# The planner of background lanes assumes a lower rate of transfers, and a higher least charge for a small one

## The chip, the cores and the metric

The kernel runs on one core of one Trainium2 chip. The metric is the device time of one execution in microseconds, and lower is better. The core has five engines that work side by side, each in the order of its own instruction stream: TensorE (PE, matmuls, with its weight loads PEld), VectorE (DVE), ScalarE (ACT), GpSimd (POOL) and SyncE (SP, which here issues nearly all transfers). Sixteen DMA engines move the data.

## The reference

One inference step of a decoder layer, for a prompt of 1024 tokens and a sample group of 8 x 4 tokens that share the weights (D_MODEL 1024, FF 2816, all f32):

```python
h = rmsnorm(x, ln1)
proj = h @ w_in          # 7432 columns, split into the inputs of three mixers and the gates
oa = attn_fn(aq, ak, av, sinks)                  # window of 128, 8 heads, 2 kv heads
cu, _ = causal_dwconv(sC * sh, sc_prev, sc_conv_w); ob = sB * cu
oc = gated_deltanet(dqkv, dz, da, db, ...)       # chunked delta rule, a recurrence over chunks
gates = sigmoid(gl)                              # three vectors of 1024 per token
merged = gates[0] * (oa @ w_br_a) + gates[1] * (ob @ w_br_b) + gates[2] * (oc @ w_br_c)
x = x + merged @ w_o
up = rmsnorm(x, ln2) @ ffn_up
gate, val = split(causal_dwconv(up, ff_prev, ffn_conv_w))
x = x + (silu(gate) * val) @ ffn_down            # then a last rmsnorm
```

The outputs are the two token groups and the new caches and states of the mixers.

## The kernel before, in words

All 1056 tokens are held with features on the partitions. Every operand of a large matmul is split into two parts of reduced width, high and low (lines 217 and 218), and a product is three matmuls. A plain projection (`proj`, line 325) makes 128 output columns: three groups of 352 tokens, each 24 matmuls into one PSUM bank of the tag `mm`, of which there are three, and then an evacuation. The larger jobs (`Pairs.run`, line 1429) make 256 output columns with seven block products in place of eight; their operands are sums and differences of blocks, built beforehand (for the gates by `h_build`, lines 1812 and 1824).

The work is one list of foreground jobs in an order written out by hand (`ORDER`):

```python
d4 hbd q0 d5 d6 dpairs d7 D0 D2 D8 D10 delta
v k q1 q2 q3 attn_in attn
sc_start c0 h0 c1 b0 h1 c2 b1 h2 c3 b2 h3 sc_end z0 z1 z2 z3 hb b3
g10 g11 g12 g13 g14 less pairs g15 G16 G00 G02 G04 G06 G20 G22 op1 G24 G26
```

Small letters are plain projections. Evacuations: `v`, `k`, `q`, `c` and `g` in line 1203 on ScalarE, `h` in line 1230 and `b` in line 1253 on VectorE, `z` in lines 1464 and 1465 on both. `G` are pair jobs of the gates. After the list come the merge of the branches, w_o, the up projection (22 jobs) and the down projection.

Everything that is no large matmul runs in background lanes: Python generators that issue a few instructions, then yield a condition. The step `delta` starts the lanes of the delta rule. `pass1` (line 796 and around it) makes 8 chunks' matrices and stores their blocks to `blk_d`, `a_d` and `qk_d`; `solve` loads `blk_d` and runs 31 pairs of VectorE instructions, one after the other (lines 828 and 830), with a yield after every eight; `merge` combines the inverses in products up to line 927; `prep` loads a chunk (six transfers of 256 KB), transposes it (lines 965 and 967) and scales it, at most two chunks ahead; `scan` carries the state through the chunks (lines 988 to 1016). `out_norm` follows (lines 605 and 613). Attention is in lanes too (lines 1601 to 1690). `hb` adds `h_build` for the gate pairs, which begins when all eight chunks are prepared and 12 attention parts are done; it ignores the planner's gate. The step `pairs` waits until `h_build` has taken its first buffers, and G16 until it has built all.

The class `Lanes` (lines 76 to 119) decides where in the program each lane step stands. It keeps a planned time `now` and the planned end of the transfers issued so far, `busy`. The helper `dma` (line 178) charges each transfer before it issues it. A foreground job calls `tick` between its matmuls; in the stretch from `rr1` on a plain projection ticks once in two matmuls with 0.36 us (line 330). A tick moves `now` and runs one step of the first lane that may run; while `busy` is more than 8 us ahead of `now` the lanes marked as moving data may not. A lane that waits for its data yields `arrived`, which is true once `now` has passed the planned end of the transfers plus 3.4 us. Where the foreground needs what a lane has not done yet, `until` runs lane steps alone, 0.3 us of planned time each, and without that gate:

```python
def arrived(self):
    return self.after(max(self.busy - self.now, 0) + DMA_US + 0.9)
def tick(self, force=False, us=TICK_US):
    self.now += us
    full = self.busy - self.now > MAX_BUSY_US and not force
```

The planner's times are only used while the program is written; the chip doesn't see them. The instructions are then ordered per engine by a list scheduler, in which a later place in the program is a lower priority, evacuations are moved up by 100 to 200 places, and an instruction whose inputs are not ready lets later ones pass. The order is fixed before the run.

Of the kernel before, what the change touches and what calls it, by code (L numbers as in the profile page):

```python
# [173 lines left out]
def trunk(tc, A, O, cst_d):  # L174
    nc = tc.nc
    bg = Lanes()

    def dma(dst, src, eng=nc.sync):
        n = 4
        for d in dst.shape:  # L180
            n *= d
        bg.transfer(max(0.5, n / 3.6e5))
        eng.dma_start(dst, src)  # L183
    done = {}

# [60 lines left out]

    ident = cp.tile([128, 128], F32, name="ident")
    dma(ident, cst_d[:, K_ID:K_ID + 128])
    ones_r = cp.tile([128, 128], F32R, name="ones_r")
    hot = cp.tile([128, 96], F32R, name="hot")  # L250
# [11 lines left out]
    def w_load(key, src, nk):  # L262
        t = cp.tile([128, 8, 128], F32, name="wr", tag="wr", bufs=2)
        dma(t[:, :nk, :], src, nc.sync)
        wraw[key] = (t, nk)
# [101 lines left out]
    def state_in(src, rows, nct, dst, name):  # L367

        n = rows * nct
        sd = dtile(name, [n, 128])  # L370
        dma(sd.rearrange("(c r) p -> c r p", r=rows), src.rearrange("r (c p) -> c r p", p=128))
        yield sb.room(1)
        full, rest = n // 128, n % 128
        st = sb.take([128, full + 1, 128])
        if full:
            dma(st[:, 0:full, :], sd[0:full * 128, :].rearrange("(i q) p -> q i p", q=128))
        if rest:
            dma(st[0:rest, full, :], sd[full * 128:n, :])
        yield bg.arrived()
        for i in range(full + (rest > 0)):  # L380
            w = 128 if i < full else rest
            ps = bg_ps()
            transpose(ps[:, :w], st[:w, i, :], ident[:w, :w])
            nc.scalar.copy(dst[:, i * 128:i * 128 + w], ps[:, :w])
            yield
        sb.drop()
# [2084 lines left out]
```

## Time and profile before

| | us |
|---|---|
| median of 3 runs (1920.84 to 1924.7) | 1923.15 |
| the profiled execution, its own time | 1918.24 |
| its span, first to last instruction | 1916.4 |
| TensorE busy | 1776.1 |
| VectorE busy | 1222.4 |
| GpSimd busy | 1116.0 |
| ScalarE busy | 825.1 |

Busy times are of the span; engines overlap. Idle time of an engine counts only where the end waits for it. A matmul row gives the time in which the group was busy; since matmuls overlap in the pipeline, the mean of one (334 ns) is longer than the distance between two.

### The profile page before, as it was taken

What the parts mean: (1) busy time and instruction counts of PE and PEld (TensorE: products, weight loads), DVE (VectorE), ACT (ScalarE), POOL (GpSimd) and SP (SyncE); (2) the same over time, 40 slices, a digit from 0 to 9 for tenths busy, and PEclk for the clock granted to TensorE, in tenths of its full rate; (3) what the DMA queues carried; (4) which work ended last, traced back from release to release, by engine and by line L of the source; (5) the groups of instructions that cost most, each with busy time, mean ns of one, the idle gap of its engine ahead of it and who ended that gap; (6) DMA issues with size and microseconds to landing.
All of it is one profiled execution on the core that took longest, in us unless ns stands there. A gap on an engine that the chain in (4) does not pass through costs nothing.

```text
span 1916.4 us, 34346 instructions
## 1 busy us (share of the span) xinstructions
PE 1776.1 (93%) x13006; PEld 1731.0 (90%) x13006; DVE 1222.4 (64%) x2122; ACT 825.1 (43%) x1780; POOL 1116.0 (58%) x1041
## 2 busy tenths in 40 slices
PE   5899989869999998999988899999999999989997
PEld 4799889769999997999987899999999999889997
DVE  5588813473477787411899956778777778764334
ACT  5445511221244543344553445554554454454433
POOL 3255623443332247976668745998887989434542
PEclk8899999987999998999999999999999999999999
DMA  6312697545765543733461343455454343596513
GB/s 221 99 46 90 192 284 217 143 120 134 183 185 158 163 131 97 264 132 117 156 242 64 134 135 129 127 163 177 142 175 147 121 143 131 224 360 194 179 51 108
DMA packets 293302, 300.84 MB, mean 157 GB/s; under 512 B 56516, under 2 KB 224944, under 8 KB 293120
## 3 DMA queue, kind: packets, MB, share of 16 engines
q1 hardware_dynamic: 233648, 261.94, 42.4%
q10 hardware_dynamic: 59488, 36.70, 6.7%
q8 instruction: 102, 1.67, 0.4%
q14 instruction: 64, 0.52, 0.1%
HBM read 205.30 MB, written 95.28 MB: 157 GB/s over the span
## 4 chain that ended last, share of the span: by engine, by line
PE 56%; DVE 18%; DMA 9%; POOL 5%; issue 5%; ACT 4%; SPq 2%; ACTq 0%; DVEq 0%; POOLq 0%
PE mm L325 15%; PE mm L1429 13%; PE bgps L1429 10%; DVE slot L360 2%; SPq L183 2%; PE bgps L2347 2%; PE bgps L2348 2%; PE bgps L2349 2%; PE mm L2348 1%; PE mm L2349 1%; PE mm L2347 1%; DVE bgps L1457 1%; POOL wl L218 1%; DVE slot L218 1%; DVE slot L2007 1%
## 5 line engine op out<-in xcount | busy, mean ns | idle before, releaser
L325 PE MATMUL mm<-slot,wh 128*128 128x352 f32 x1920 | 488.5, 334 | 40.4 <-DVE slot L1253 21.8
L325 PEld LDWEIGHTS mm<-slot,wh 128*128 128x128 f32 x1920 | 345.2, 194 | 47.5 <-DVE slot L1253 22.0
L325 PE MATMUL mm<-slot,wl 128*128 128x352 f32 x960 | 319.5, 333 | 4.0 <-POOL wl L218 4.0
L1429 PE MATMUL mm<-slot,wh 128*128 128x264 f32 x1536 | 213.6, 289 | 15.6 <-DVE bgps L1457 6.3
L1429 PEld LDWEIGHTS mm<-slot,wh 128*128 128x128 f32 x1536 | 199.5, 192 | 20.5 <-DVE bgps L1457 8.2
L1429 PE MATMUL mm<-slot,wl 128*128 128x264 f32 x1464 | 202.9, 288 | 12.3 <-DVE wl L218 4.2
L1429 PEld LDWEIGHTS mm<-slot,wl 128*128 128x128 f32 x1464 | 188.7, 191 | 15.5 <-DVE wl L218 5.0
L218 POOL TENSOR_TENSOR wl<-slot,wl 128x512 fp32r<-128x512 f32 (+1 forms) x116 | 153.4, 1322 | 83.1 <-ACT wl L217 70.4
L325 PEld LDWEIGHTS mm<-slot,wl 128*128 128x128 f32 x960 | 186.3, 194 | 6.5 <-POOL wl L218 4.7
L218 POOL TENSOR_TENSOR wh<-slot,wh 128x512 fp32r<-128x512 f32 (+1 forms) x103 | 133.7, 1299 | 95.9 <-ACT wh L217 76.0
L218 POOL TENSOR_TENSOR slot<-slot 128x512 fp32r<-128x512 f32 (+3 forms) x95 | 136.0, 1436 | 88.4 <-ACT slot L217 88.2
L217 ACT CAST slot<-slot 128x528 fp32r<-128x528 f32 (+4 forms) x212 | 130.6, 638 | 126.4 <-DVE slot L1824 32.5
L218 POOL TENSOR_TENSOR wl<-wr,wh 128x1024 fp32r<-128x1024 f32 x38 | 94.6, 2489 | 144.0 <-ACT wh L217 134.8
L218 DVE TENSOR_TENSOR slot<-slot 128x528 fp32r<-128x528 f32 (+3 forms) x117 | 115.5, 1002 | 90.3 <-ACT slot L217 83.9
L1429 PE MATMUL bgps<-slot,wl 128*128 128x264 f32 x1128 | 154.1, 287 | 8.2 <-POOL wl L218 4.8
L1429 PEld LDWEIGHTS bgps<-slot,wl 128*128 128x128 f32 x1128 | 144.9, 190 | 9.7 <-POOL wl L218 5.0
L1429 PE MATMUL bgps<-slot,wh 128*128 128x264 f32 x1080 | 146.8, 286 | 2.6 <-DVE slot L2007 1.2
L1429 PEld LDWEIGHTS bgps<-slot,wh 128*128 128x128 f32 x1080 | 138.6, 191 | 3.5 <-DVE slot L2007 1.7
L2187 DVE SCALAR_TENSOR_TENSOR bgps<-slot,bgps 128x358 f32<-128x358 f32 x240 | 127.3, 590 | 13.7 <-ACT bgps L2185 13.0
L1429 PE MATMUL mm<-slot 128*128 128x264 f32 x936 | 124.6, 284 | 1.2 <-DVE bgps L1457 0.6
L217 ACT CAST wl<-slot 128x512 fp32r<-128x512 f32 (+1 forms) x128 | 74.2, 583 | 108.0 <-PE bgps L1429 29.2
L1429 PEld LDWEIGHTS mm<-slot 128*128 128x128 f32 x936 | 118.0, 188 | 1.9 <-DVE bgps L1457 0.8
(404 smaller groups left out, 3929.7 us busy)
## 6 DMA issues: line engine op xcount, KB each, us to landing
wr<-in_w_in SPq DMA_DIRECT2D x32, 512.0 KB
g_d<-slot SPq DMA_DIRECT2D x24, 528.0 KB
slot<-g_d SPq DMA_DIRECT2D x24, 528.0 KB
ht_d<-slot SPq DMA_DIRECT2D x44, 264.0 KB
slot<-ht_d SPq DMA_DIRECT2D x44, 264.0 KB
wr<-in_ffn_up ACTq DMA_DIRECT2D x22, 512.0 KB
slot<-in_ffn_down SPq DMA_DIRECT2D x22, 512.0 KB
slot<-in_ffn_up ACTq DMA_DIRECT2D x22, 512.0 KB
```

What stands on the lines that cost most here:

```text
L183: eng.dma_start(dst, src)
L217: nc.scalar.copy(hi, src)
L218: eng.tensor_tensor(lo, src, f32(hi), op=ALU.subtract)
L325: mm(ps[:, :TG], a[:, k, :], b[k][:, cc], start=n == 0, stop=n == last)
L360: nc.vector.scalar_tensor_tensor(out[:, :L], src[:, j:j + L], w(j), out[:, :L], op0=ALU.mult, op1=ALU.add)
L1429: mm(ps, w[:, x + k, :], b[y][:, c0:c0 + HU], start=not n and piece not in NESTED, stop=n == last, skip_group_check=piece in NESTED)
L1457: nc.vector.tensor_tensor(dst, ps, x, op=ALU.add)
L2007: nc.vector.scalar_tensor_tensor((acc if b == 1 else g)[:, cc], g[:, cc], 1.0, ps, op0=ALU.add, op1=ALU.mult)
L2187: nc.vector.scalar_tensor_tensor(ps, cb[:, a + i:b + i], w(i), ps, op0=ALU.mult, op1=ALU.add)
L2347: mm(ps, hi, bh, start=start, stop=False, skip_group_check=True)
L2348: mm(ps, hi, bl, start=False, stop=False, skip_group_check=True)
L2349: mm(ps, lo, bh, start=False, stop=stop, skip_group_check=True)
```

## The change

One line of the helper `dma`. Nothing that is computed, no instruction and no buffer is changed by it; the charge of a transfer of n bytes is.

```diff
@@ -179,7 +179,7 @@
         n = 4
         for d in dst.shape:
             n *= d
-        bg.transfer(max(0.5, n / 3.6e5))
+        bg.transfer(max(0.6, n / 2.8e5))
         eng.dma_start(dst, src)
     done = {}
```

`bg.transfer` is `self.busy = max(self.busy, self.now) + us`.

## Rows read from the trace of the kernel before

**Rows 1.** The page: busy time of engines, and the span in 40 slices.
```profile
PE 1776.1 (93%) x13006; PEld 1731.0 (90%) x13006; DVE 1222.4 (64%) x2122; ACT 825.1 (43%) x1780; POOL 1116.0 (58%) x1041
...
PE   5899989869999998999988899999999999989997
...
PEclk8899999987999998999999999999999999999999
```

**Rows 2.** Waits of TensorE, whole span: us in total, times, longest.
```profile
PE mm L325 <- DVE slot L1253: 21.8, 1, 21.8
PE mm L325 <- ACT slot L1203: 10.9, 2, 8.1
```

**Rows 3.** Table by stretch: length, busy us of PE, PEld, DVE, ACT, POOL, PEclk, DMA share, GB/s.
```profile
219.00:506.00 287.00, 249.28 (x1521) 238.37 (x1520) 117.14 (x240) 63.86 (x137) 111.79 (x100) 0.91 0.70 189
240.00:290.00 50.00, 43.34 (x250) 42.48 (x251) 7.55 (x15) 7.93 (x14) 13.18 (x6) 0.91 0.98 283
...
436.00:480.00 44.00, 44.00 (x267) 43.59 (x266) 10.96 (x22) 6.52 (x12) 15.01 (x14) 0.81 0.62 138
480.00:510.00 30.00, 30.00 (x187) 27.22 (x187) 8.24 (x15) 7.94 (x13) 9.62 (x9) 0.95 0.76 194
506.00:690.00 184.00, 182.69 (x1259) 176.90 (x1260) 134.47 (x255) 83.75 (x215) 56.68 (x40) 1.00 0.59 166
...
720.00:750.00 30.00, 20.52 (x104) 18.72 (x103) 29.93 (x19) 9.84 (x18) 25.48 (x12) 0.81 0.21 73
```

**Rows 4.** Lines 1253, 927, 965 and 1203: where foreground and delta lanes stand.
```profile
502.00 0.49 DVE L1253 TENSOR_TENSOR slot<-mm,slot 128x320 f32<-128x320 f32 x1 [0.93 <-PE mm L325]
511.47 0.53 DVE L1230 TENSOR_TENSOR slot<-mm,slot 128x352 f32<-128x352 f32 x1 [1.30 <-PE mm L325]
...
L927 PE MATMUL bgps<-slot x32: 218/275/275, 502.3 to 505.7; 128*128 128x64 f32 x32
...
L965 PE MATMUL bgps<-ident,slot x32: 270/272/273, 518.9 to 688.5; 128*128 128x128 f32 x32
...
634.75 0.82 ACT L1203 ACTIVATE slot<-mm 128x352 f32<-128x352 f32 x2
687.42 0.47 ACT L1203 ACTIVATE slot<-mm 128x352 f32<-128x352 f32 x1
745.93 1.16 ACT L1203 ACTIVATE slot<-mm 128x352 f32<-128x352 f32 x3
```

**Rows 5.** DMA issues from 219 to 506 us: count, KB each.
```profile
wr<-in_w_in SPq DMA_DIRECT2D x17, 512.0 KB
qkv_d<-slot SPq DMA_DIRECT2D x11, 512.0 KB
slot<-qkv_d SPq DMA_DIRECT2D x19, 256.0 KB
slot<-rows_d SPq DMA_DIRECT2D x17, 256.0 KB
slot<-ssq_d SPq DMA_DIRECT2D x8, 528.0 KB
slot<-raw_d SPq DMA_DIRECT2D x7, 528.0 KB
...
blk_d<-slot SPq DMA_DIRECT2D x32, 16.0 KB
...
a_d<-slot SPq DMA_DIRECT2D x16, 16.0 KB
```

**Rows 6.** Building of the gate operands, and line 325 alone by stretch (PE, PEld, PEclk, DMA).
```profile
689.86 2.45 POOL L1812 TENSOR_TENSOR slot<-slot 128x1056 f32<-128x1056 f32 x1
...
750.61 1.81 DVE L1824 TENSOR_TENSOR slot<-slot 128x528 f32<-128x528 f32 x1
...
219.00:506.00 287.00, 194.87 (x1083) 182.31 (x1083) 0.91 0.70 189
219.00:690.00 471.00, 312.62 (x1741) 288.02 (x1742) 0.95 0.65 180
690.00:750.00 60.00, 35.67 (x205) 34.16 (x204) 0.91 0.31 100
```

**Rows 7.** The solve on VectorE, and waits between 380 and 450 us.
```profile
398.50 0.19 DVE L828 TENSOR_TENSOR slot<-slot 128x31 f32<-128x31 f32 x1 [2.37 <-DMA slot<-blk_d]
...
433.60 0.19 DVE L828 TENSOR_TENSOR slot<-slot 128x31 f32<-128x31 f32 x1
...
DVE slot L828 <- DMA slot<-blk_d: 2.4, 1, 2.4
...
POOL wl L218 <- DMA slot<-a_d: 9.1, 1, 9.1
```

**Rows 8.** Table by stretch, late stages; columns as in group 3.
```profile
1070.00:1680.00 610.00, 589.46 (x4599) 584.68 (x4597) 460.88 (x868) 296.42 (x649) 472.94 (x510) 0.99 0.45 149
1680.00:1900.00 220.00, 215.83 (x1758) 213.81 (x1759) 100.35 (x160) 93.76 (x180) 95.56 (x76) 0.99 0.56 186
```

## The prediction

> **What bounds it now.** I read the page first [rows 1]: TensorE is busy 93% of 1916.4 us, its clock is granted at 9 or better in most slices, and the slices that fall short are the first, those around 240 to 290 and 410 to 480 us, 720 to 770 us, and the last. So time is lost in a few places, and the question is which of them the pacing reaches. The waits of TensorE [rows 2] put the largest single wait, 21.8 us, on the evacuation in line 1253 (VectorE). The table by stretch [rows 3] sizes the rest: from 219 to 506 us TensorE is busy 249.28 of 287 us at a clock of 0.91 (1.0 is 2.4 GHz, a stretch at 1.2 GHz counts as 0.5), from 506 to 690 it is full (182.69 of 184), and from 720 to 750 it is busy 20.52 of 30 while VectorE is busy 29.93.
>
> The order of this program around the change is made ahead of time: every foreground tick moves the planner's clock (0.36 us for two matmuls here, so 12.96 for a projection job of 72) and runs one lane step, but no moving lane while the planned backlog of transfers is over 8 us. That backlog is what the edit makes larger. It changes no instruction, only where lane steps stand among the foreground jobs.
>
> **The change, step by step.** A 528 KB transfer goes from 1.50 to 1.93 planned us, 512 KB from 1.46 to 1.87, 256 KB from 0.73 to 0.94, anything up to 128 KB from 0.50 to 0.60.
>
> *Step 1, how late the delta lanes get.* The delta chain (pass1, solve, merge) ends with line 927 at 505.7 us, in the foreground between the last evacuation of b2 (502.00) and the first of h3 [rows 4]. From the delta step that is 15 jobs, 15 x 12.96 = 194 planned us. The transfers issued in this stretch (56 groups in the view, 289 transfers, 53.8 MB; eight groups stand) [rows 5] cost 218 planned us by the old rule and 273 by the new: 174 of them are small (+0.1 each, +17), the rest adds 37. More transfer time than foreground time means that the gate at 8 us is what admits lanes here, so the 55 us fall mostly on the lanes. The trace doesn't show the gate itself. Upper bound: all 55, and some 15 more in the preparation that follows (48 loads of 256 KB, +0.21 each, and attention's) = 70. Lower bound: the gate is open half the time, 25. I take 45, nearer the upper end, because the sum exceeds the room.
>
> *Step 2, the slack that hides it.* The last preparation (lines 965, 967, at 689 us) stands just behind the third evacuation of g12 (687.42) [rows 4]: from 634.75 to 745.93 there are 18 evacuations in line 1203, six jobs g10 to g15, and this is the ninth. So 24 of the 26 jobs before the step `pairs` are done; two jobs, 25 planned us, are slack. Delays up to that cost nothing: the matmuls of g13 and g14 only change places with lane work. With 45 the planner stands at `pairs` and runs lanes alone for 20 us; all foreground that is left to put beside them is g15, and behind it G16 waits for the same lane h_build.
>
> *Step 3, what the lost cover costs.* From 690 to 750 us the operands of the gate pairs are built (lines 1812 and 1824, 689.86 to 750.61), and TensorE's cover there is 35.67 us of line 325, 205 matmuls, that is g13 to g15 [rows 6]. Put ahead of the preparation, two of the three are gone: 35.67 x 2/3 = 24 us of idle time, if the building takes as long as now (VectorE fills it, [rows 3], so I see no reason for it to shrink much). The 20 planned us ahead of it are 1.4 chunks of the preparation (one per 24.2 us now: 169.6 us from the first to the last line 965, seven steps [rows 4]). Of a chunk's 24.2 us foreground takes 15.5 (117.75 of 182.69 busy us from 506 to 690, line 325 [rows 3, 6]); alone, a chunk runs on its own chain, between 8.7 us (its TensorE work, no idle) and 24.2 (nothing faster, 15.5 idle). I take 4.5 idle, nearer the lower end since most of the chunk's time is foreground, so 6. The wait also brings a low clock: 720 to 750 stands at 0.81 [rows 3], 4 us on 20.52; I take 4 more. Step 3: +34 us, with 0 (delay within the slack) and 35.67 + 2 x 15.5 = 67 as ends.
>
> *Step 4, what comes back.* From 240 to 290 us the DMA engines are at 0.98 and move 283 GB/s; TensorE loses 6.66 us, and 3.9 to a clock of 0.91 [rows 3]. Lanes that ask for less per us should leave that stretch free: -10.6 (0 to -10.6). The 21.8 us wait is a different thing: the solve (lines 828 and 830, 398.50 to 434 us) runs on VectorE without a break because its input landed late (2.4 us waited for blk_d, and GpSimd 9.1 us for a load of a_d [rows 7]), while TensorE had already filled its three banks with b1. With the clock after it (0.81 over 44 us, 8.4, and 0.95 over 30, 1.5 [rows 3]) this place costs 32 us. The edit leaves the four bursts of the solve in consecutive lane steps, so the lump stays, somewhere else in the order; but with DMA less crowded it may come on time. Between 0 and -32 I take a third, -11: the landing is a small part of the lump.
>
> *Step 5, elsewhere.* From 1070 us on the DMA engines are at 0.45 and 0.56 [rows 8], so the larger waits for arrival (0.2 to 0.4 us each) lie under matmuls: 0. If lane work does come late there, the cover is gone and some us go; I allow 5 either way. At the end `drain` ignores the gate: 0, at most 1.
>
> Sum: +34 - 10.6 - 11 = +12 us. The profiled execution took 1918.24 us (span 1916.4), which gives 1930; the median of the runs shown is 4.9 us above that execution, so I forecast **1935** against 1923.15.
>
> The rate itself can be held against the rows: 283 GB/s at 0.98 [rows 3] says that 280 KB per us is what this mix of transfers gets, and that 360 is not reached there. The Trainium skill (DMA: Bandwidth & Descriptors, Specifications) states about 358 GB/s as a core's limit to HBM, which is the old figure. By that, step 4 would be 0, the sum +34 and the time 1957; the measured stretch decides, for it is the mix that is paced.
>
> **Rivals.**
> - *The stall goes.* The solve falls beside a job that ScalarE evacuates, or its input is on time. Then -32 instead of -11, and with the smaller loss of step 3 (one job of cover, 12, +4 clock): 16 - 10.6 - 32 = -27, about 1897 by the median; with step 3 at 34 it is -9, 1914. For it: 32 us stand in one place and the DMA is overfull ahead of it. Against it: solve's steps stay together, and b and h jobs, two in three, need VectorE to evacuate.
> - *Nothing moves.* The delay stays within 25 planned us and the solve's stall stays: within 4 us of 1923.
> - *Full loss.* The wait at `pairs` is 45 planned us, the stall keeps its size: up to 67 - 10.6 = +56, 1979; half way, with 45, 1958. It decides once the gate is shut all through 219 to 506.
>
> **How the numbers follow.** Forecast (slower, own range 1928 to 1950) 0.45; stall gone 0.34; nothing 0.10; full loss 0.11. A difference of 0.2%, 4 us, is about what a measurement of this kernel can tell from none. Faster 0.34, same 0.10, slower 0.56. The range takes in most of the first rival's times and half of the last: 1896 to 1966.
>
> **What would show it.** Right: the last line 967 stands behind the evacuations of g14 rather than g12; TensorE is busy under 15 us of the 30 before the first line 1429; the DMA share around 240 to 290 us falls below 0.9. Wrong: no idle stretch ahead of the first gate pair (the slack was larger than I count), or the wait on line 1253 and the low clock behind it are gone without another VectorE lump in their place, which would make it faster.

## The result, and the profile after

| | us |
|---|---|
| changed kernel, median of 20 runs (1922.83 to 1938.42) | 1932.85 |
| kernel before, median of 20 runs (1914.27 to 1924.7) | 1920.52 |
| ratio, with its 95% interval | 1.0063 [1.0053, 1.0074] |
| the changed kernel's profiled execution | 1923.49 |

The change makes the kernel slower by 12 us. The forecast was +12 (1935 against 1923.15). The profiled execution of the changed kernel is the second fastest of its 20 runs, so its trace, 5.3 us over that of before (1923.49 against 1918.24), shows less than the median's loss; the other 7 us stand in no trace.

The page of the changed kernel: busy time, the span in 40 slices, and what the DMA engines moved.

```profile
PE 1778.9 (93%) x13006; PEld 1732.0 (90%) x13006; DVE 1226.4 (64%) x2122; ACT 826.7 (43%) x1780; POOL 1122.6 (58%) x1041
...
PE   5899999997999974999998899999999999989997
...
PEclk7899999999899986999998999999999999999999
...
GB/s 216 102 47 90 189 273 195 125 172 129 142 179 187 134 130 106 210 193 138 155 201 114 112 146 113 149 128 160 171 142 144 150 128 164 222 354 210 181 52 108
```

Against [rows 1] the work is the same to the instruction (13006 matmuls), but the weak slices have moved: the 6 at 383 to 431 us is a 9, the slice behind it, a 9 before, is a 7, and the two slices from 673 to 769 us, 9 and 8 before, now stand at 7 and 4; the clock's row has its 6 at the last of these. (A slice is 48 us.) The waits of TensorE over the whole span say the same (us in total, times, longest):

```profile
PE bgps L613 <- ACT slot L217: 16.0, 3, 14.2
...
PE mm L325 <- DVE slot L1465: 10.5, 1, 10.5
```

The 21.8 us on line 1253 [rows 2] is gone as such; behind the solve there now stands one of 10.5, on the evacuation of a z job (line 1465). New is 14.2 us on line 613, the sums of `out_norm`. That is lane work; the wait ends at 748.93 us, and TensorE runs nothing in it, no foreground either. The table by stretch (columns as in [rows 3]) sizes both places.

```profile
219.00:506.00 287.00, 268.08 (x1663) 258.92 (x1662) 137.66 (x264) 72.05 (x160) 119.82 (x102) 0.96 0.67 184
240.00:290.00 50.00, 48.84 (x308) 48.15 (x307) 15.43 (x18) 12.48 (x24) 13.43 (x5) 1.00 0.91 274
...
450.00:480.00 30.00, 19.49 (x114) 19.09 (x113) 28.83 (x63) 5.79 (x17) 10.04 (x9) 0.85 0.36 100
480.00:510.00 30.00, 30.00 (x179) 29.21 (x178) 6.81 (x14) 6.78 (x13) 7.72 (x7) 0.81 0.58 143
...
506.00:690.00 184.00, 177.13 (x1192) 169.52 (x1191) 100.63 (x186) 70.03 (x172) 48.87 (x36) 0.98 0.61 165
690.00:771.00 81.00, 47.12 (x281) 42.46 (x282) 76.16 (x98) 33.40 (x75) 42.84 (x24) 0.71 0.32 102
771.00:954.00 183.00, 180.37 (x1473) 179.28 (x1473) 64.66 (x88) 81.45 (x167) 142.15 (x102) 1.00 0.49 170
...
741.00:771.00 30.00, 12.95 (x49) 10.41 (x50) 29.55 (x23) 10.23 (x17) 18.58 (x9) 0.50 0.19 74
```

The kernel before, in the two stretches that answer to the last ones:

```profile
690.00:750.00 60.00, 50.52 (x302) 48.16 (x302) 56.85 (x54) 24.73 (x49) 41.97 (x19) 0.91 0.31 100
750.00:944.00 194.00, 188.73 (x1508) 187.50 (x1507) 64.65 (x89) 83.11 (x171) 143.74 (x106) 0.98 0.47 164
```

From 219 to 506 us TensorE idles 18.9 us, 37.7 before [rows 3], at a better clock: calmer, as hoped. From 690 to 771 it idles 34 us with the clock at 0.71, while VectorE is busy 76 of 81; before, it was 9.5 us from 690 to 750. The positions tell why (rows of lines, as in [rows 4] and [rows 6]):

```profile
558.18 0.49 DVE L1253 TENSOR_TENSOR slot<-mm,slot 128x320 f32<-128x320 f32 x1 [9.35 <-PE mm L325]
...
L927 PE MATMUL bgps<-slot x32: 218/275/275, 553.6 to 557.0; 128*128 128x64 f32 x32
...
L965 PE MATMUL bgps<-ident,slot x32: 270/272/421, 575.4 to 725.1; 128*128 128x128 f32 x32
...
647.55 0.46 ACT L1203 ACTIVATE slot<-mm 128x352 f32<-128x352 f32 x1
725.81 1.18 ACT L1203 ACTIVATE slot<-mm 128x352 f32<-128x352 f32 x3
...
707.79 3.40 POOL L1812 TENSOR_TENSOR slot<-slot 128x1056 f32<-128x1056 f32 x1
...
769.17 0.69 DVE L1824 TENSOR_TENSOR slot<-slot 128x528 f32<-128x528 f32 x1
```

The chain's products in line 927 end beside b3, job 21 (558.18 is its third evacuation), not b2, job 15. The evacuations of g14 are through at 647.55, and the last preparation comes at 725.1, 78 us later; the only foreground job evacuated after g14 is g15 (725.81, three at once). The gate operands are built from 707.79 to 769.17, where 689.86 to 750.61 stood [rows 6]. The pair jobs' evacuations in line 1489 end the gates; here in the kernel before and then in the changed one:

```profile
L1489 ACT ACTIVATE slot<-mm x18: 368/381/394, 770.3 to 943.3; 128x264 f32<-128x264 f32 x18
```

```profile
L1489 ACT ACTIVATE slot<-mm x18: 368/384/395, 788.9 to 953.7; 128x264 f32<-128x264 f32 x18
```

So 10.4 us are lost by then. From this point to the end the two profiled executions take 974.5 and 969.4 us, and the experiments' 969 to 975, in no order that follows the planned waits below. So the later stages move a single execution by some 6 us, and what the pacing decides is to be looked for ahead of them.

### The profile page after: what moved, and what is told of

It is laid out like the page before. It is cut to its first block, busy times and chain, and to the rows that moved or that the text cites. A ratio compares the mean times of both kernels' runs of the same rounds, so it can differ in the third digit from the quotient of the medians.

```text
span 1921.7 us, 34338 instructions
## 1 busy us (share of the span) xinstructions
PE 1778.9 (93%) x13006; PEld 1732.0 (90%) x13006; DVE 1226.4 (64%) x2122; ACT 826.7 (43%) x1780; POOL 1122.6 (58%) x1041
## 5 line engine op out<-in xcount | busy, mean ns | idle before, releaser
L1429 PEld LDWEIGHTS mm<-slot,wh 128*128 128x128 f32 x1536 | 200.9, 193 | 24.4 <-ACT slot L1438 11.2
L218 POOL TENSOR_TENSOR wl<-slot,wl 128x512 fp32r<-128x512 f32 (+1 forms) x116 | 158.4, 1365 | 69.0 <-ACT wl L217 64.1
L218 POOL TENSOR_TENSOR slot<-slot 128x512 fp32r<-128x512 f32 (+3 forms) x95 | 138.7, 1465 | 79.0 <-ACT slot L217 79.0
L218 POOL TENSOR_TENSOR wl<-wr,wh 128x1024 fp32r<-128x1024 f32 x38 | 94.2, 2479 | 154.6 <-ACT wh L217 149.7
L217 ACT CAST wh<-wr 128x1024 fp32r<-128x1024 f32 (+2 forms) x88 | 67.4, 772 | 124.4 <-PE mm L325 70.5
```

What stands on the lines that cost most here:

```text
L217: nc.scalar.copy(hi, src)
L218: eng.tensor_tensor(lo, src, f32(hi), op=ALU.subtract)
L1429: mm(ps, w[:, x + k, :], b[y][:, c0:c0 + HU], start=not n and piece not in NESTED, stop=n == last, skip_group_check=piece in NESTED)
```

## The experiments

My theory: the lanes stand later among the foreground jobs, use up the foreground that covered the building of the gate operands, and the tail (the stretch from 506 us to the end of the gate pairs) loses more than the calmer stretch from 219 to 506 us saves. Rivals: any wait of the planner costs the same (A), the order changes by chance (B), later stages lose (C), plain jobs are simply better (D), the crowded transfers make the solve stall (E). "Planned" times are those of the code's own clock, worked out by its rule for each kernel. Two sizes are read in each trace: TensorE's idle time from 219 to 506 us, and from 506 to the end of the gate pairs (last line 1489). They come from one profiled execution each, the ratios from all runs. Four pairs of kernels have the same order up to the end of the first stretch (before and e6, changed and e5, e1 and e10, e2 and e7); their idle times there differ by 0.6 to 4.1 us, which is how far one trace can be trusted.

| | planned wait ahead of G16 | idle 219 to 506 | idle 506 to end of gates | gates end at | ratio [interval] |
|---|---|---|---|---|---|
| before | 0 | 37.7 | 16.1 | 943.7 | 1 |
| changed | 64 + 15 | 18.9 | 43.4 | 954.1 | 1.0063 [1.0053, 1.0074] |
| e1 rate only | 38 + 15 | 31.1 | 37.9 | 957.0 | 1.0040 [1.0028, 1.0052] |
| e2 least charge only | 7 + 14 | 16.1 | 26.3 | 937.5 | 0.9944 [0.9927, 0.9962] |
| e3 new, delta to `less` | 47 + 14 | 22.6 | 52.1 | 966.1 | 1.0113 [1.0096, 1.0130] |
| e4 new, elsewhere | 0 + 6 | 35.9 | 19.8 | 944.8 | 0.9986 [0.9966, 1.0006] |
| e5 changed, more cover | 19 + 15 | 23.0 | 27.5 | 944.6 | 0.9977 [0.9962, 0.9993] |
| e6 before, more cover | 0 | 36.2 | 14.8 | 938.9 | 0.9982 [0.9968, 0.9997] |
| e7 e2, more cover | 0 | 15.2 | 12.8 | 922.2 | 0.9876 [0.9852, 0.9901] |
| e8 changed, gate at 20 | 66 + 15 | 29.3 | 43.2 | 972.1 | 1.0113 [1.0092, 1.0135] |
| e9 e6, solve spread | 0 | 26.0 | 11.9 | 925.8 | 0.9916 [0.9890, 0.9942] |
| e10 e1, more cover | 0 + 7 | 30.5 | 18.6 | 932.0 | 0.9919 [0.9899, 0.9938] |
| e11 e7, solve spread | 0 + 5 | 11.5 | 20.5 | 913.1 | 0.9807 [0.9788, 0.9827] |

**Each half of the edit alone (e1, e2).**

```diff
-        bg.transfer(max(0.5, n / 3.6e5))
+        bg.transfer(max(0.5, n / 2.8e5))     # e1
+        bg.transfer(max(0.6, n / 3.6e5))     # e2
```

> Rate 280 KB per us, small transfers still at 0.5. My theory: the loss is the planned wait ahead of the gate pairs (lanes alone at `pairs` and at G16), less what the calmer stretch from 219 to 506 us saves. Planned wait here 38 + 15 = 53 us against 64 + 15 = 79 in the changed kernel and 0 before, so the tail loses about two thirds of the 36 us that the changed kernel's trace shows, 24, and the saving of 30 stays: ratio to before 0.997 to 1.004. Rival A (any wait there costs the same, since it is the building of the gate operands that is uncovered): 1.005 to 1.008. Rival B (chance of the order, no relation to the wait): anything in 0.99 to 1.01.

> Least charge 0.6, rate still 360. Planned wait 7 + 14 = 21 us. My theory: tail loss about a quarter to a half of 36 (9 to 18), and part of the saving (half of 30): ratio 0.996 to 1.002. Rival A: 1.005 to 1.008 as soon as the planner waits at all. Rival B: 0.99 to 1.01 without relation to the wait.

Measured: 1928.39 us (ratio 1.0040), at the top of my range, and 1912.01 us (0.9944), below it. The halves differ in sign. e1 doesn't separate my theory (up to 1.004) from Rival A (from 1.005); e2 does. The tables by stretch, e1 and then e2:

```profile
219.00:506.00 287.00, 255.93 (x1589) 247.19 (x1588) 131.62 (x261) 69.41 (x155) 113.44 (x100) 0.93 0.64 179
506.00:957.00 451.00, 413.06 (x3007) 400.24 (x3007) 235.72 (x374) 187.32 (x416) 237.20 (x163) 0.95 0.52 158
```

```profile
219.00:506.00 287.00, 270.91 (x1627) 260.59 (x1625) 144.48 (x268) 67.92 (x154) 118.58 (x102) 0.92 0.66 184
506.00:937.50 431.50, 405.25 (x2979) 395.01 (x2979) 236.25 (x370) 188.74 (x419) 229.91 (x161) 0.96 0.52 162
...
240.00:290.00 50.00, 43.70 (x267) 42.84 (x267) 10.71 (x19) 11.29 (x22) 15.18 (x7) 0.98 1.00 300
```

In idle time e2 keeps the whole saving of the first stretch, with little over a third of the tail's extra idle time (26.3, between 16.1 and 43.4). With the low clock counted (0.92 there), it saves 22 us of the 31 that the changed kernel does. e1 saves little ahead (it still has a wait of 19.2 us on line 1253 behind its solve) and loses in the tail. So the tail grows with the planned wait, and Rival A falls by e2; but what the first stretch saves doesn't go with the charge. Nor is it relief of the DMA engines: e2 has them at 1.00 from 240 to 290 us, busier than before, and is the faster kernel.

**Where the new charge acts (e3, e4).**

```diff
+        on = done.get("dl") and not done.get("pr")   # set by the steps delta and less
-        bg.transfer(max(0.5, n / 3.6e5))
+        bg.transfer(max(0.6, n / 2.8e5) if on else max(0.5, n / 3.6e5))   # e3; e4 the other way
```

> The new charge only from the step `delta` to the step `less` (just ahead of `pairs`), the old one before and after. Planned wait 47 + 14 = 61 us. My theory: the whole effect is here, ratio 1.002 to 1.008, first gate pair as late as in the changed kernel. Rival C (the loss comes from later stages, where arrivals are waited for longer): 0.998 to 1.001.

> The complement: the new charge everywhere but from `delta` to `less`. Planned wait 0 + 6 us. My theory: within 0.997 to 1.002 of before, with the wait of about 22 us on line 1253 still in the trace. Rival C: 1.004 to 1.008.

Measured: 1942.26 us (1.0113), above my range, and 1916.66 us (0.9986, its interval touches 1). The loss comes from the stretch between `delta` and `pairs`, and Rival C falls. But e3 loses 9 us more than the whole change, with a shorter planned wait, so the order also has a part that no planned wait tells: Rival B is not ruled out for differences of that size. The tail of e3:

```profile
506.00:966.10 460.10, 408.00 (x2945) 393.88 (x2944) 232.04 (x372) 183.79 (x412) 233.52 (x162) 0.94 0.50 152
```

The wait behind the solve is 16.7 us in e4, where I had expected the 22 us on line 1253, and 13.0 in e3, both on the evacuation of an h job. From 240 to 290 us, first e4, then e3:

```profile
240.00:290.00 50.00, 50.00 (x317) 49.60 (x316) 18.67 (x19) 11.84 (x23) 13.29 (x5) 1.00 1.00 301
...
240.00:290.00 50.00, 47.33 (x289) 47.03 (x290) 9.78 (x19) 11.64 (x21) 15.82 (x7) 0.97 1.00 302
```

e4 has the old charge in this stretch, and the DMA engines are full, yet TensorE loses nothing there; e3 has the new one and idles 2.7 us. So the new charge isn't needed in this stretch to free it. In the kernel before, 3.9 of the 6.7 idle us are one wait of a lane's matmul (line 796) for its load from `qkv_d`; e2 has that wait here too (5.3 us), the changed kernel, e3 and e4 don't.

**More cover (e5, e6, e7).** The first gate pairs are made as plain jobs and put ahead of the wait. A plain job needs no built operands.

```diff
-g10 g11 g12 g13 g14 less pairs g15 G16 G00 G02 G04 G06 G20 G22 op1 G24 G26
+g10 g11 g12 g13 g14 g15 g16 g17 g00 less pairs g01 G02 G04 G06 G20 G22 op1 G24 G26   # e5
+g10 g11 g12 g13 g14 g15 g16 less pairs g17 G00 G02 G04 G06 G20 G22 op1 G24 G26       # e6, e7
```

> The changed kernel, with the gate pairs G16 and G00 made as four plain jobs g16, g17, g00, g01, so that the step `pairs` comes three jobs later and two plain jobs stand between it and the first pair. 144 matmuls of 352 columns in place of 168 of 264 per pair cost about 2.8 us each, 5.6 in all. My theory (the tail loses because foreground that covered the building has been used up): planned wait 19 + 15 us in place of 64 + 15, so about half of the 36 us of tail loss comes back, net -8 to -20: ratio to before 0.996 to 1.002. Rival A (the chain itself is slower under the new charge, cover or not): 1.006 to 1.010, that is, the changed kernel plus 3 to 6 us.

> Control: the kernel before with its old charge, G16 made as g16 and g17, `pairs` after g16. There is no planned wait to cover. My theory: +2.8 us for the plain jobs, less at most the 10 us that TensorE now idles from 720 to 750 us: ratio 0.996 to 1.002. Rival D (plain jobs are simply better here, whatever the charge): under 0.995.

> The least charge of 0.6 alone (rate 360) with G16 made as g16 and g17 and `pairs` after g16. The planned waits of 7 and 14 us are gone. My theory: the saving of about 22 us from 219 to 506 us stays, of the extra 18 us of tail waste most comes back less 2.8: ratio 0.985 to 0.992, the best so far. Rival A: 0.995 to 0.998, the gain of the least charge less the price of the plain jobs.

Measured: 1915.01 us (0.9977), 1917.05 (0.9982) and 1894.97 (0.9876), each within its range. The same kind of edit (four plain jobs in e5, two in e6 and e7) is worth 18 us to the changed kernel (1932.85 to 1915.01) and 17 to e2 (1912.01 to 1894.97), which wait, and 3 to the kernel before (0.18%), which doesn't; by the ratios it is 16, 13 and 3. Most of it stands in the tail, whose idle time falls by 16 us in e5 and 13 in e7. That is the tail's loss and its cause shown: lost cover. Rivals A and D fall. e7, from 506 us on, and its cover at 720 to 750, where e2 idled 17 of 30 us at a clock of 0.54:

```profile
506.00:922.20 416.20, 403.36 (x2967) 393.78 (x2965) 237.72 (x364) 184.47 (x410) 229.33 (x154) 1.00 0.54 168
...
720.00:750.00 30.00, 23.43 (x150) 21.79 (x148) 26.51 (x17) 8.17 (x15) 22.03 (x11) 1.00 0.28 93
```

```profile
720.00:750.00 30.00, 13.04 (x54) 10.44 (x55) 27.16 (x22) 10.97 (x19) 18.02 (x9) 0.54 0.23 88
```

The first fence is e7, the second e2.

**The gate (e8).**

```diff
-TICK_US, UNTIL_US, DMA_US, MAX_BUSY_US = 0.45, 0.3, 2.5, 8.0
+TICK_US, UNTIL_US, DMA_US, MAX_BUSY_US = 0.45, 0.3, 2.5, 20.0   # on the changed kernel
```

> The changed kernel with the gate at 20 planned us of backlog in place of 8. If the gate is what makes the lanes late (as I had it), the chain's products in line 927 come earlier by 20 us or more and the loss shrinks: 0.998 to 1.003. If it is the planned queue itself, through `arrived`, line 927 stands within 10 us of the changed kernel's 557 and the ratio stays at 1.003 to 1.010.

Measured: 1941.31 us (1.0113), a little above the range I gave the second case, and the chain's products end where they did (557.0) or later:

```profile
L927 PE MATMUL bgps<-slot x32: 217/275/275, 562.4 to 567.4; 128*128 128x64 f32 x32
```

The gate is not what makes the lanes late. Raised to 20, it lets the backlog grow longer, and `arrived`, which waits for the planned end of all transfers issued, takes the time that the gate gave: by the planner's rule the charges made from the step `delta` to the end of the chain fill 179 of 186 planned us in the kernel before, 256 of 260 in the changed kernel and 258 of 263 in e8. What bounds the lanes in this stretch is the planned queue itself.

**The solve (e9), and two more combinations (e10, e11).**

```diff
-            if j % 8 == 7:
-                yield
+            if j % 2 == 1:
+                yield bg.after(0.7)      # e9 on e6, e11 on e7
```

> Old charge and the order of e6 (g16, g17 plain, `pairs` after g16); the solve yields after every two of its 31 pairs and lets 0.7 planned us pass, so that its VectorE instructions are no longer one lump in the order. My theory: the wait of about 22 us of TensorE in the solve, and the low clock behind it, together about 32 us, go away, and the later chain (19 planned us) is covered by the two jobs: ratio 0.982 to 0.990 against 0.998 of e6. Rival E (the stall is due to the crowded transfers ahead of it, not to the lump): the wait stays or comes back on another line, 0.994 to 1.000.

> The rate of 280 alone (least charge 0.5) with the four plain jobs of e5. Planned wait 6.6 us at the first pair in place of 38 + 15. My theory: of the 7.8 us that e1 lost against before, the tail's share comes back less 5.6 for the plain jobs: ratio 0.986 to 0.996. Rival A: 1.005 to 1.009.

> e7 (least charge 0.6, g16 and g17 plain) with the spread solve of e9. In e7 the solve already stands beside jobs that pass between its instructions, so my theory gives little: 0.984 to 0.990 against 0.9876. If the low clock from 219 to 506 us of e7 (0.91) comes from the solve, 0.975 to 0.984.

Measured: 1908.49 us (0.9916), 1905.23 (0.9919, within its range) and 1884.52 (0.9807). The profiled executions of e6 and e9 are the fastest of theirs, 8 and 12 us under their medians. In e9 the wait behind the solve, 21.5 us in e6, is 5.0; first e6, then e9:

```profile
PE mm L325 <- DVE slot L1253: 21.5, 1, 21.5
```

```profile
PE mm L325 <- DVE slot L1253: 5.0, 1, 5.0
```

So the lump makes the stall, under the old charge and with the old crowd of transfers, and Rival E falls. But the gain is 0.66% of 1920 (0.9982 less 0.9916), 12.7 us, not 32: e9 misses its range, since idle time from 219 to 506 falls by 10 us only (36.2 to 26.0) and the solve, now spread, puts the chain behind it later (line 927 ends at 513.1 us, 504.1 in e6). e10 gives the rate's half its cover back (gates end 25 us earlier than in e1) and comes out ahead of before with a wait of 19.8 us behind the solve still in it. e11 is the fastest kernel here, 36.5 us under the kernel before in the same round. My theory (0.984 to 0.990) had it too slow; the number lies in the second case:

```profile
219.00:506.00 287.00, 275.52 (x1726) 264.10 (x1724) 142.12 (x277) 74.17 (x166) 125.66 (x106) 0.97 0.71 195
506.00:913.10 407.10, 386.60 (x2851) 379.29 (x2851) 224.01 (x352) 176.50 (x396) 219.32 (x150) 0.97 0.52 163
```

Its clock from 219 to 506 us is 0.97, 0.91 in e7, as that second case asks. Whether the spread solve does that or the rest of the new order wasn't tried.

## Why the prediction was right, step by step

The sign and the size came out as forecast, +12 against +12. Later lanes and lost cover, the mechanism named for the loss, are shown by e3 to e7. The stretch ahead became calmer too, but not for the reason given, and that the size fits so well is partly luck: the delay, the wait and the price of a us of it were each off, and the errors cancel. The traces don't show +12 either: steps 3 and 4 come to +36 and -31 in them, 4 us more go to a lower clock ahead of 219 us (0.91 for 0.93; e5, with the same order up to there, has 0.94, so it is likely chance), which makes the 10 us that the gates end later, and the last stretch gives 5 back. By its steps (the loss of a stretch is its length less busy time times granted clock, added up from the tables piece by piece, good to some 3 us):

- *Step 1, the delay: too small.* I took 45 planned us with 70 as the upper end; the chain's products moved by nearly six jobs, up to 6 x 12.96 = 78. What failed is the reading of the gate. I took it for what admits the lanes, some of the time, and so took less than the full 55. By e8 the planned queue itself is the bound, and by the planner's rule its charges up to the end of the chain grow by 77 us: 44 for the same 253 transfers at the new charge, and 33 for 25 transfers more, most of that six of 512 KB and seven of 528 KB, the sizes of the foreground's own. The jobs that pass while the chain is late lengthen the queue in which it waits; that I had not counted.
- *Step 2, the slack: right* in kind. Two jobs, 25 planned us, were to spare; e4, which waits 6 planned us, is no slower, and roughly, with e3 out of order, the kernels that wait longer idle longer in the tail.
- *Step 3, the loss of cover: +34 forecast, +36 in the trace, but wrong in its factors.* The planner waits 64 us at `pairs` where I had 20, but a us of that wait costs less than I charged. Up to 690 us the loss rose by 9 (6 forecast): the preparation of a chunk took 21.4 us instead of 24.2 (149.7 us over seven steps), and TensorE still idled only 6.9 of 184. While the operands are built, idle time rose by 24.4 us (9.5 to 33.9; 24 forecast), and the low clock, 0.71 for 0.91, took 9 more (4 forecast). The gate pairs behind gave 6 back (9 to 3), which no step had.
- *Step 4, what comes back: -21.6 forecast, -31 in the trace* ((287 - 249.28 x 0.91) less (287 - 268.08 x 0.96), 60.2 less 29.6). From 240 to 290 us: -10.6 forecast, -9.4 found (idle 1.2, clock 1.00). The place of the solve cost 32 us with its clock; now it costs 10.5 and 9 for the clock (0.85 and 0.81 from 450 to 510 us), 13 less, where I had taken 11. The rest, about 8 us, is other time that I hadn't counted. But neither reason holds up. The kernels at 280 KB per us throughout do load the DMA engines less from 240 to 290 us and idle little there (changed, e1, e5, e8, e10: 0.91 to 0.96, 0.0 to 3.7 us), yet e4 idles 0.0 under the old charge with the engines full, so that lower demand frees the stretch isn't shown. And the wait behind the solve doesn't follow the crowd of transfers: it is 21.8 before, 19.2 in e1, 16.7, 13.0 and 10.5 in e4, e3 and the changed kernel, and no wait of that kind is left in e2, whose DMA engines are at 1.00 from 240 to 290 us. What seems to count is which jobs stand beside the solve in VectorE's order; e9 takes most of the wait away by breaking the lump.
- *Step 5, later stages: no loss.* 969 to 975 us from the end of the gates to the end, in every kernel; 5 less in the changed kernel's trace than before, where I allowed 5 either way.
- *The rate.* e2 keeps 360 KB per us and gains. So the figure that fits the measured 283 GB/s better is not the better figure for the planner. Nor was 283 the most that this mix gets: e2, e3 and e4 move 300 to 302 GB/s in the same 50 us. The Trainium skill (DMA: Bandwidth & Descriptors, Specifications) states about 358 GB/s as a core's limit to HBM. The slice at 1682 us, in the down projection, moves 354, but the trace of e2 doesn't agree with it as a limit, with 366 over 48 us:

```profile
1677.00:1725.00 48.00, 46.41 (x364) 45.60 (x364) 32.30 (x40) 23.98 (x43) 20.50 (x16) 0.96 1.01 366
```

Of the marks set beforehand, the last line 965 did pass g14. The share of the DMA engines from 240 to 290 us, 0.91, stayed just above the 0.9 I had asked for. The third did not come as I had worded it: the gates' first line 1429 stands at 726.3 us, beside lanes that are still at work, and in the 30 us ahead of it TensorE was busy 21.68, not under 15. The empty stretch lies behind it, ahead of the pairs that run without a break: 12.95 of 30 from 741 to 771 us, at a clock of 0.50.

```profile
696.33:726.33 30.00, 21.68 (x150) 19.96 (x149) 28.09 (x52) 13.86 (x36) 9.58 (x7) 0.89 0.38 112
```

## What to carry to other kernels

A constant of a planner that writes the order of a program is not to be set by the bandwidth it names, but by what stands where afterwards: read from the profile how many jobs of slack a chain of lanes has before the step that needs it, and work out in the planner's own time how far the edit moves it. When a chain is paced more slowly, move work that doesn't depend on it to where it will be waited for; the same charge lost 0.6% without that cover and gained 0.2% with it. And look for a long run of instructions on one engine that other engines need between: spreading it was worth some 12 us.

## What I had not expected of the hardware

DMA engines at full share need not cost TensorE anything. In e4 they are at 1.00 and move 301 GB/s from 240 to 290 us, and TensorE is busy 50.00 of the 50 us at a clock of 1.00. I had read that stretch of the kernel before, at 0.98, as a loss of 10.6 us to be won by asking for less. e2, at 1.00, still idles 6.3 us there, and by the medians it is 8.5 us faster than before all the same.
